# Two-part preparation of the delta rule's chunks, merged loads and a later front, in a two-block kernel

## The chip, the cores and the metric

The kernel runs on one core of one Trainium2 chip, as one launch. The metric is the device time in microseconds from the first to the last instruction, with what lies around it; the core's engines are TensorE (PE, with its weight loads as PEld), VectorE (DVE), ScalarE (ACT), GpSimd (POOL) and SyncE (SP), which issues all DMAs of this kernel.

## What is computed

Two blocks on 1024 tokens of width 1024. The first (a gated delta rule, a dilated attention and a feed-forward part) is the same in both kernels. The second runs twice (two layers), on 256 context and 1024 latent tokens, and is where the change lies:

```python
def _layer(x, ctx, ...):
    h_lat = x * (1.0 + scale) + shift          # the context alike
    ru, rg, aq, ak, av, ag, nq, nk, nv, ng = split(h @ w_in)
    # RWKV-7 on centred conv of ru, forward and backward, 6 heads of 64
    #   S = S*w - (S kk) b + v k;  y = S r
    S_f, S_b, ys_c = _rwkv_bidir(rin_c, S0, S0)
    _, _, ys_l = _rwkv_bidir(rin_l, S_f, S_b)
    yr = _rwkv_output(...)                     # group norm, plus bonus * v
    ya = _block_attention(...)                 # 6 query heads, 2 key heads
    yn = _neighbourhood_attention(...)         # 8 x 16 windows plus context
    y = concat(yr*silu(rg), ya*silu(ag), yn*silu(ng)) @ w_out
    x = _layer_norm(ALPHA * x + gate * y, ln_g, ln_b)
```

The inputs and results are float32. Large products are made from a rounded part and its remainder (three matmuls for one product).

## The kernel before, in words

For each layer, front makes the projections. project computes 10 blocks of 128 recurrent channels: the products land in banks "mm", are evacuated by copies that alternate between ScalarE and VectorE into raw, go through a convolution of three steps on VectorE (cv) and are stored to R in DRAM. For the third of each group of blocks (k) it also makes unit vectors kn at once: squares (sq), a product with hsel (L1356), GpSimd's power (hrs), a broadcast (L1372) and VectorE's product. Beside it factors, a generator of which project takes four steps for each block from the fifth on, works in six slices of 640 tokens: it loads X4 from R, makes tanh factors (L1576, L1578), cumulated decays, and stores the chunks' factors bk and G and the bonus vb (product at L1616). What is left of it is run in project_att. The compiler's scheduler sets the order there.

In stage the order of TensorE, VectorE, ScalarE and GpSimd is the one in which the code writes them: Timeline.run picks, among generators that wait, the one to write next, by its own account of what each engine has done (spend). SP's order is not held to it; the scheduler places the DMAs. The generators are the gate products, attention's scores and values, and the recurrence: scan walks ten steps s, each of a forward and a backward block of 128 tokens, in half-steps of 64, and needs three preparations prep(s, pr), one for each pair of heads. Data of a step lie in one of two slots (G, SK, AB, BT, U).

A prep takes one of four tickets, loads bk, G and vT into the slot (30 DMAs a step), multiplies bk with G (L1889, L1891), masks the results into A, AB and G's other half (L1893 to L1897), adds flips (L149) and inverts A in tri_inverse2: C goes to DRAM (wD) and comes back spread over partitions (wR), GpSimd does 15 steps of forward substitution of two operations each (L436, L438) and the last placing (L440), and TensorE, ScalarE and VectorE join the 16-blocks in five products (L149 to L485). The result is U. launch(s + 2) at the end of step s starts the next three that use this slot.

Attention asks for each query's raw tile with four loads (both, L2064) and for the bias with two.

## Time and profile before

| | us |
|---|---|
| median of 3 runs | 4374.69 |
| lowest, highest | 4362.69, 4382.45 |
| the profiled execution | 4353.97 |
| its span, first to last instruction | 4352.2 |
| TensorE busy in it | 3928.2 |
| mean granted clock of TensorE | 0.948 of full speed |

The granted clock has two levels, 1.2 and 2.4 GHz, shown as 0.5 and 1.0. Block 1 takes up to about 1587 us; then come, for layer 0, the recurrent projection (1668 to 1893), the other projections (to 2085), the gate products with the first preparations (to 2230), the stage of scan and attention (to 2880 and its tail to 2921) and the closing; for layer 1 the same from 3080, with its stage from 3600 to about 4218. A busy TensorE is not TensorE at its peak: a matmul counts as busy at either clock.

### The profile page before, as it was taken

The numbers are of one execution on the slowest core, as the hardware profiler recorded it, in microseconds if no ns is written. First come the engines' busy times: TensorE is split into PE (matmuls) and PEld (weight loads), VectorE is DVE, ScalarE is ACT, GpSimd is POOL, SyncE is SP. The second block draws the span as 40 slices with busy tenths as digits, with TensorE's granted clock in tenths as the row PEclk, the third lists the DMA queues.
The fourth block names the chain that finished last, engine by engine and source line by source line (L and its number), as shares of the span: only waits on it lengthen the run. The fifth ranks groups of instructions, "written<-read, shape, count | busy, mean of one in ns | idle before, by whom it ended". The sixth has DMA issues, their size and how long they took to land.

```text
span 4352.2 us, 91620 instructions
## 1 busy us (share of the span) xinstructions
PE 3928.2 (90%) x36914; PEld 3184.2 (73%) x36914; DVE 2170.0 (50%) x4701; ACT 1451.1 (33%) x2831; POOL 1698.6 (39%) x3201
## 2 busy tenths in 40 slices
PE   8989998999999998979878988899898997998988
PEld 6767777977788877658766766679766875776768
DVE  5634332489212246765235545567576524555546
ACT  4244443421111122331124544452233114554442
POOL 2444333442232234453114443436444323453435
PEclk9999999999999998989989999999998998998989
DMA  3343224445111124453332333454345334234444
GB/s 113 113 139 85 81 74 126 137 149 160 46 45 53 44 71 135 158 192 102 87 92 66 86 73 87 102 160 137 123 159 201 86 94 103 71 75 94 110 106 156
DMA packets 523961, 466.87 MB, mean 107 GB/s; under 512 B 66416, under 2 KB 448656, under 8 KB 523408
## 3 DMA queue, kind: packets, MB, share of 16 engines
q1 hardware_dynamic: 523536, 461.02, 36.3%
q8 instruction: 289, 4.73, 0.5%
q14 instruction: 136, 1.11, 0.1%
HBM read 330.43 MB, written 130.43 MB: 106 GB/s over the span
## 4 chain that ended last, share of the span: by engine, by line
PE 30%; DMA 9%; DVE 7%; POOL 4%; issue 4%; ACT 2%; SPq 1%; POOLq 0%; DVEq 0%; ACTq 0%
PE bank L687 3%; PE bank L744 3%; PE bank L723 3%; DMA wR<-wD 3%; PE bank L243 2%; PE bank L244 2%; PE bank L245 2%; PE bank L1533 1%; PE bank L149 1%; PE bank L1535 1%; PE bank L1534 1%; POOL wX L438 1%; POOL wY L436 1%; DMA wD<-wC 1%; DMA X<-R 1%
## 5 line engine op out<-in xcount | busy, mean ns | idle before, releaser
L154 POOL TENSOR_TENSOR wlo<-wraw,whi 128x1024 fp32r<-128x1024 f32 (+3 forms) x134 | 319.6, 2400 | 560.9 <-ACT whi L153 525.9
L436 POOL TENSOR_TENSOR wY<-wR,wX 128x60 f32<-128x60 f32 (+5 forms) x900 | 233.0, 259 | 428.5 <-DMA wR<-wD 375.9
L691 DVE CUSTOM_DVE_ANT_0 S<-bank,zero 128x256 f32<-128x256 f32 (+1 forms) x372 | 204.7, 558 | 173.6 <-PE bank L687 170.9
L727 ACT COPY PT<-bank 128x512 f32<-128x512 f32 x346 | 202.0, 584 | 236.4 <-PE bank L723 234.4
L153 ACT CAST whi<-wraw 128x1024 fp32r<-128x1024 f32 (+3 forms) x164 | 156.9, 989 | 370.0 <-PE bank L245 163.0
L245 PE MATMUL bank<-h2T,wlo 128*128 128x512 f32 x704 | 278.1, 397 | 0.0
L244 PE MATMUL bank<-h2T,whi 128*128 128x512 f32 x704 | 277.9, 395 | 0.0
L243 PE MATMUL bank<-h2T,whi 128*128 128x512 f32 x704 | 275.9, 394 | 0.3 <-ACT h2T L785 0.3
L438 POOL TENSOR_TENSOR wX<-wX,wY 128x60 f32<-128x60 f32 (+5 forms) x900 | 237.6, 264 | 70.5
L243 PE MATMUL bank<-whi,yh 128*128 128x256 f32 x832 | 241.4, 291 | 17.7 <-ACT yh L153 16.1
L723 PE MATMUL bank<-cst,S 128*128 128x128 f32 x1416 | 233.6, 288 | 19.4 <-ACT S L648 10.2
L244 PE MATMUL bank<-wlo,yh 128*128 128x256 f32 x832 | 240.5, 289 | 3.2 <-DVE wlo L2257 2.8
L744 PE MATMUL bank<-PT,nav 128*64 128x128 f32 (+1 forms) x2832 | 239.4, 290 | 3.4 <-ACT PT L727 3.2
L245 PE MATMUL bank<-whi,yl 128*128 128x256 f32 x832 | 239.5, 289 | 0.8 <-POOL yl L154 0.8
L648 ACT ACTIVATE S<-S,mx 128x1280 f32<-128x1280 f32 (+3 forms) x180 | 202.9, 1127 | 10.3 <-DVE mx L695 8.5
L723 PEld LDWEIGHTS bank<-cst,S 128*128 128x128 f32 x1416 | 161.2, 143 | 57.7 <-ACT PT L727 17.7
L744 PEld LDWEIGHTS bank<-PT,nav 128*64 128x64 f32 (+1 forms) x2832 | 152.2, 139 | 69.3 <-issue 51.8
L415 POOL TENSOR_TENSOR wB<-A,cst 128x256 f32<-128x256 f32 x60 | 43.9, 732 | 406.4 <-DVE A L1893 406.4
L243 PE MATMUL bank<-hT,whi 128*128 128x512 f32 x464 | 190.1, 410 | 10.4 <-ACT sqkv L131 6.7
L244 PE MATMUL bank<-hT,whi 128*128 128x512 f32 x464 | 187.0, 403 | 0.0
L245 PE MATMUL bank<-hT,wlo 128*128 128x512 f32 x464 | 186.0, 401 | 0.0
L1332 DVE CUSTOM_DVE_ANT_0 mj<-wm,cc 128x512 bf16<-128x512 f32 x192 | 179.3, 934 | 8.4 <-POOL cc L1320 3.2
(467 smaller groups left out, 10877.2 us busy)
## 6 DMA issues: line engine op xcount, KB each, us to landing
wraw<-in_w_in SPq DMA_DIRECT2D x86, 512.0 KB
wR<-wD SPq DMA_DIRECT2D x60, 512.0 KB
wm<-in_w_mod SPq DMA_DIRECT2D x96, 256.0 KB
X<-R SPq DMA_DIRECT2D x12, 1280.0 KB
G<-gt SPq DMA_DIRECT2D x24, 640.0 KB
bk<-bk SPq DMA_DIRECT2D x24, 640.0 KB
bk<-bk SPq DMA_DIRECT2D x120, 128.0 KB
G<-G SPq DMA_DIRECT2D x240, 64.0 KB
```

Source lines behind the costliest of these rows:

```text
L154: (eng or self.nc.gpsimd).tensor_tensor(lo, raw, hi.bitcast(F32), ALU.subtract)
L243: nc.tensor.matmul(p, lhsT=lh, rhs=rh, start=kk == 0, stop=False)
L244: nc.tensor.matmul(p, lhsT=lh, rhs=rl, start=False, stop=False)
L245: nc.tensor.matmul(p, lhsT=ll, rhs=rh, start=False, stop=kk == n - 1)
L436: eng.tensor_tensor(t, custom(R, i * 64 + i + 1, [((15 - 2 * i) * 64 + 31 - i, 2), (16, 2), (1, n)]), custom(x, i, [(47 - 2 * i, 2), (16, ...
L438: eng.tensor_tensor(o, o, t, ALU.subtract)
L648: nc.scalar.activation(s[:, :total], s[:, :total], AF.Exp, bias=mx[:, 5:6], accum_out=mx[:, 6:7])
L691: nc.vector.tensor_tensor_reduce(out=s[:, c0:c0 + n], in0=p[:, c0 % 512:c0 % 512 + n], in1=b, scale=1.0, scalar=-3.0e38, op0=ALU.add, op1= ...
L723: nc.tensor.transpose(pt[:rows[i], i], P[h][0][:, c0:c0 + rows[i]], k.ident)
L727: nc.scalar.copy(t[:, :full], pt[:, :full])
L744: nc.tensor.matmul(pv[h * 64:h * 64 + 64, 0], lhsT=V, rhs=t[:V.shape[0], i], start=seen[h] == 1, stop=seen[h] == n)
L1332: nc.vector.tensor_tensor_reduce(out=j, in0=w, in1=cc[:, v, i * 512:i * 512 + 512], scale=1.0, scalar=0.0, op0=ALU.mult, op1=ALU.add, accu ...
```

## The change

- prep is in two parts. Part one takes a ticket, loads bk in one DMA and gk, a second copy of G's columns of 128 partitions, in one, into the tile that wR takes afterwards; multiplies bk with the first half of gk (L1942), masks it into A, and inverts A in its own place. Part two waits for the slot (ready[s]), copies A to U on ScalarE, makes the other products (L1956, L1958), the masks and the flips, and gives the ticket back.
- shared(s) loads a slot's G and vT for all three pairs of heads in 10 DMAs; fill(s + 2) starts it at the end of step s, and the first time in rwkv. The preparations of the next step are launched when the third of a step has its ticket.
- In tri_inverse2 the store of C, the load of wR and GpSimd's steps are steps of the planner of their own.
- The planner counts 0.6 us of SP for each DMA, a queue of 220 KB/us that all share, and 1.8 us after it; before it counted 0.06, 2.0 and 120 KB/us for each alone.
- A query's raw tile takes two loads, a pair of bias tiles one; the query's next load, the stores of attention's results and of the gates each have a step of their own.
- Front: the unit vectors are spread over the next blocks (unit) and written into sq; all evacuations in project go to ScalarE; five tiles t5 instead of four; factors takes the fourth channel block as a tile of its own, leaves each slice's bonus to the next slice, and has banks "f" (6 and 7) while "r" keeps 4 and 5; three of its steps for each block instead of four.

The core of the diff:

```diff
 def project(...):
+    def unit(pr, a, sq):
+        yield
+        norms = heads_rsqrt_bc(k, hp, sq, 0, NT, 1.0, "max", 1e-12, slow=True)
+        next(norms)
+        yield
+        for b0, m, p in norms:
...
+        nc.sync.dma_start(L.R[:, pr * 4 + 2, :], sq[:, 0:1280])
...
-            k.copy(raw[:, o:o + n], p)
+            nc.scalar.copy(raw[:, o:o + n], p)
         dn.chan(w, j % 2 * 128, hT, segs, ev)
+        next(norm, None)
...
-            for _ in range(4):
+            for _ in range(3):
                 next(side, None)
 def tri_inverse2(...):
     nc.vector.tensor_reduce(C, ...)
+    yield "-"
     nc.sync.dma_start(D.rearrange("b j x -> (b j) x"), C.rearrange("p u t -> p (u t)"))
-    R = new("R", (128, 16, 4, 16), 0)
-    nc.sync.dma_start(R, ...)
     eng.tensor_copy(x, ...)
-    yield "-", 1.0
+    yield "-"
+    R = new("R", (128, 16, 4, 16), 0)
+    nc.sync.dma_start(R, ...)
+    yield "-"
 Timeline.spend:
-            t = max(self.at[e], self.now)
-            self.at[e] = t + 0.06
-            self.landed = max(self.landed, t + 2.0 + math.prod(c for _, c in i.outs[0].ap) * 4 / 120e3)
+            t = self.at[e] = max(self.at[e], self.now) + 0.6
+            t = self.at["queue"] = max(self.at["queue"], t) + math.prod(c for _, c in i.outs[0].ap) * 4 / 220e3
+            self.landed = max(self.landed, t + 1.8)
 def rwkv(...):
-    def prep(s, pr):
+    def shared(s):
+        a = s % NS
+        f, b = fwd[s], bwd[s]
+        for h in range(2):
+            for pr in range(3):
+                nc.sync.dma_start(G[a][h][HS[h], pr].rearrange("p (d c) x -> p d (c x)", d=2),
+                                  two(L.G[HS[h], pr, 0, 0, :], f * 256, b * 256, 20 * 128, [(1, 256)]))
+            for d, blk in ((0, f), (1, b)):
+                nc.sync.dma_start(SK[a][h][HS[1 - h], :, 0, d * 2:d * 2 + 2]..., L.vT[:, :, h, blk * 2:blk * 2 + 2]...)
+        yield "-"
+        ready[s] = True
+    def prep(s, pr):
...
         ticket = tickets.pop(0)
+        started[s] += 1
+        if started[s] == 3:
+            launch(s + 1)
...
-                nc.tensor.matmul(p[HS[h], u], lhsT=be[u][HS[h]], rhs=g[h][HS[h], pr, u], start=True, stop=True)
+                nc.tensor.matmul(p[HS[h], u], lhsT=be[u][HS[h]], rhs=gk[HS[h], u, 0:64], start=True, stop=True)
+        A = t1(f"A{ticket}", (128, 4, 64))
+        nc.vector.tensor_tensor(v4(A), v4(p), rm[:, :, :, 0:64], ALU.mult)
+        yield "-"
+        yield from tri_inverse2(k, wk, A, A, ticket, nc.gpsimd)
+        yield "-"
+        while not ready[s]:
+            yield WAIT
+        nc.scalar.copy(U[a][:, pr], A)
+        yield "B", 0.0, None, ("mm", "g")
...
-        rounds.add(flips(a, pr, be, ka), 1 + s * 0.05)
-        yield "-"
-        yield from tri_inverse2(k, wk, A, U[a][:, pr], ticket, nc.gpsimd)
+        yield from flips(a, pr, be, ka)
         tickets.append(ticket)
...
-            launch(s + 2)
+            fill(s + 2)
```

How the order moves, at three places. First SP in layer 0, early in the stage. The numbers behind a name are the buffer: G00 and G01 are slot 0's, refilled for step 2, G10 and G11 slot 1's; wR2 as the output of a load from G0 is gk. Before:

```order
L423 DMA wD_17169<-wC_17167 128x64
L425 DMA wR_17171<-wD_17169 128x1x1024
L2064 DMA qraw_17198<-gqk0_12533 64x128 x4
L2138 DMA ydr0_12536<-rsum_17215 128x128
L423 DMA wD_17238<-wC_17236 128x64
L1879 DMA bk0_18148<-bk0_12537 128x2x128 x2
L425 DMA wR_17240<-wD_17238 128x1x1024
L1879 DMA bk2_18682<-bk0_12537 128x2x128
L1881 DMA G00_15641<-G0_12538 64x256
L1881 DMA G01_15642<-G0_12538 64x256
```

After, from behind a value tile, three vv, a second value tile and the first bias tile:

```order
L2256 DMA nab_23989<-in_rpb 128x2x512
L1932 DMA bk0_16979<-bk0_12537 128x2x256
L1913 DMA G10_16931<-G0_12538 64x2x256 x3
L1916 DMA SK10_16929<-vT0_12531 64x3x128 x2
L1913 DMA G11_16932<-G0_12538 64x2x256 x3
L1916 DMA SK11_16930<-vT0_12531 64x3x128 x2
L1932 DMA bk2_16952<-bk0_12537 128x2x256
L1935 DMA wR2_16954<-G0_12538 128x2x256
L1932 DMA bk3_16956<-bk0_12537 128x2x256
L1935 DMA wR3_16958<-G0_12538 128x2x256
L1935 DMA wR1_17316<-G0_12538 128x2x256
L2183 DMA qraw_17131<-gqk0_12533 64x2x128 x2
L1913 DMA G00_15653<-G0_12538 64x2x256 x3
```

The G of slot 0 stood behind two pairs of wD and wR; now the loads of two slots follow each other, six or ten in one stretch, and the loads that part one needs (bk and gk) stand between them with no wD or wR ahead.

Second TensorE in the same place: the first product of the third preparation that uses slot 0 or, after, of a preparation ahead of its slot. Before:

```order
L744 MATMUL bank4_75<-PT_17404,nav_16845 64x128 x4
L1889 MATMUL bank0_71<-G00_15641,bk3_17376 64x128
L1889 MATMUL bank0_71<-G01_15642,bk3_17376 64x128
L1891 MATMUL bank5_76<-G00_15641,bk3_17376 64x128
L1891 MATMUL bank5_76<-G01_15642,bk3_17376 64x128
```

After:

```order
L748 MATMUL bank4_75<-PT_17252,nav_16927 64x128 x4
L752 MATMUL bank4_75<-cst_63,mx_17217 64x128
L752 MATMUL bank4_75<-cst_63,mx_17223 64x128
L1942 MATMUL bank0_71<-wR2_16954,bk2_16952 64x64 x8
L150 MATMUL bank6_77<-cst_63,bk1_16539 64x64 x2
```

The product that A is made from read G00 and G01 of the slot; it now reads wR2, which is gk, and the flips of another preparation follow it.

Third TensorE at the end of layer 0's recurrent projection (kd0 the bonus, sq and hrs the unit vectors, cv the transposes of v, w2s the tanh factors). Before:

```order
L1576 MATMUL bank6_77<-hid_13075,w2s_13074 128x320 x2
L1616 MATMUL bank4_75<-kd0_13489,cst_63 128x320
L1616 MATMUL bank5_76<-kd0_13489,cst_63 128x320
L1576 MATMUL bank4_75<-hid_13075,w2s_13074 128x320
L1576 MATMUL bank5_76<-hid_13075,w2s_13074 128x320
L1356 MATMUL bank4_75<-cst_63,sq_13730 128x2 x10
L1372 MATMUL bank5_76<-cst_63,hrs_13743 64x128 x8
L1372 MATMUL bank6_77<-cst_63,hrs_13743 64x128 x8
L1372 MATMUL bank4_75<-cst_63,hrs_13743 64x128 x4
L1425 MATMUL bank2_73<-cst_63,cv_13908 128x128 x4
L1425 MATMUL bank3_74<-cst_63,cv_13908 128x128 x2
L1576 MATMUL bank5_76<-hid_13075,w2s_13074 128x320
```

After:

```order
L1587 MATMUL bank6_77<-kd0_13580,cst_63 128x320
L1377 MATMUL bank5_76<-cst_63,hrs_13811 64x128 x3
L1587 MATMUL bank7_78<-kd0_13580,cst_63 128x320
L1377 MATMUL bank5_76<-cst_63,hrs_13811 64x128 x5
L1377 MATMUL bank4_75<-cst_63,hrs_13811 64x128 x3
L1447 MATMUL bank2_73<-cst_63,cv_13815 128x128 x2
L1377 MATMUL bank4_75<-cst_63,hrs_13811 64x128 x2
L1608 MATMUL bank6_77<-hid_13075,w2s_13074 128x320
L1377 MATMUL bank4_75<-cst_63,hrs_13811 64x128 x3
L246 MATMUL bank1_72<-whi_13940,hA01_12151 128x256
L244 MATMUL bank1_72<-whi_13940,hA00_12150 128x256
```

Before, the product with hsel (sq) and its broadcast (hrs) follow each other; after, the product with hsel has gone up among the projection's products, and the broadcast is followed by such products (L246, L244).

## Rows read from the trace of the kernel before

**Rows 1.** The page, part 1: busy us (share of the span) xinstructions.
```profile
PE 3928.2 (90%) x36914; PEld 3184.2 (73%) x36914; DVE 2170.0 (50%) x4701; ACT 1451.1 (33%) x2831; POOL 1698.6 (39%) x3201
```

**Rows 2.** Windows, the projection's two tails: us, engines' busy (xcount), PEclk, DMA share, GB/s.
```profile
1850.50:1895.00 44.50, 24.11 (x104) 15.46 (x102) 27.59 (x32) 13.41 (x23) 25.16 (x16) 0.62 0.55 194
...
3262.00:3305.00 43.00, 25.54 (x116) 17.28 (x115) 27.95 (x31) 10.76 (x20) 24.65 (x16) 0.64 0.54 188
```

**Rows 3.** Windows, gate products and stage of layer 0, then of layer 1.
```profile
2085.00:2230.00 145.00, 133.59 (x1083) 109.30 (x1081) 30.63 (x62) 23.65 (x49) 28.79 (x99) 0.96 0.28 78
2230.00:2880.00 650.00, 548.16 (x9868) 435.87 (x9869) 337.26 (x1131) 305.09 (x669) 262.37 (x915) 0.93 0.36 89
3486.00:3600.00 114.00, 106.76 (x828) 82.97 (x827) 28.87 (x53) 21.35 (x41) 28.00 (x99) 0.97 0.32 92
3600.00:4240.00 640.00, 563.44 (x9841) 444.28 (x9842) 337.36 (x1109) 308.36 (x647) 271.17 (x919) 0.93 0.38 92
```

**Rows 4.** Waits of PE, recurrent projection, project_att, layer 1's projection: us, times, longest.
```profile
PE bank L243 <- DVE raw L133: 6.9, 2, 5.6
...
PE bank L1616 <- DVE kd L1613: 4.4, 3, 1.7
...
PE bank L1356 <- ACT sq L1433: 5.4, 1, 5.4
```

**Rows 5.** Waits of PE in both stages: 2085:2230, then 2230:2880, then 3600:4240.
```profile
PE bank L149 <- POOL wR L440: 6.3, 1, 6.3
...
PE bank L1889 <- DMA G<-G: 26.2, 7, 16.2
...
PE bank L149 <- issue: 9.6, 1, 9.6
PE bank L149 <- POOL wR L440: 9.1, 3, 5.3
PE bank L149 <- DVE G L1897: 7.6, 3, 3.8
...
PE bank L149 <- POOL wR L440: 16.3, 3, 8.4
PE bank L1889 <- DMA G<-G: 6.2, 6, 2.2
```

**Rows 6.** SP in order of time: start us, us, line, operation, tiles.
```profile
2271.19 0.38 SPq L423 DMA_DIRECT2D wD<-wC  x1
2276.72 0.63 SPq L425 DMA_DIRECT2D wR<-wD  x1
...
2286.45 1.74 SPq L1881 DMA_DIRECT2D G<-G  x3
```

**Rows 7.** PE in order of time, in brackets the idle us before and its end.
```profile
2293.86 0.65 PE L1889 MATMUL bank<-G,bk 64*64 64x128 f32 x2 [16.21 <-DMA G<-G]
```

**Rows 8.** The loads of G in layer 0's stage: duration ns min/median/max.
```profile
L1881 SPq DMA_DIRECT2D G<-G x108: 444/588/1408, 2234.2 to 2760.5; - x108
```

**Rows 9.** Groups of PE, 3600:4218: shape, xcount | busy us, mean ns | idle.
```profile
L1889 PE MATMUL bank<-G,bk 64*64 64x128 f32 x432 | 34.5, 287 | 6.3 <-DMA G<-G 6.2
...
L149 PE MATMUL bank<-cst,wR 64*64 64x64 f32 x432 | 19.0, 230 | 17.3 <-POOL wR L440 16.3 <-issue 0.9
```

**Rows 10.** SP's own waits, 2230:2880.
```profile
SPq L2138 <- DVE rsum L756: 44.5, 12, 13.9
...
SPq L425 <- DMA wD<-wC: 39.2, 20, 5.7
```

**Rows 11.** The page, part 5: xcount | busy, mean ns | idle before, releaser.
```profile
L436 POOL TENSOR_TENSOR wY<-wR,wX 128x60 f32<-128x60 f32 (+5 forms) x900 | 233.0, 259 | 428.5 <-DMA wR<-wD 375.9
...
L438 POOL TENSOR_TENSOR wX<-wX,wY 128x60 f32<-128x60 f32 (+5 forms) x900 | 237.6, 264 | 70.5
```

**Rows 12.** Groups of ACT, 1668:1893 and 2230:2880.
```profile
L129 ACT COPY raw<-bank 128x512 f32<-128x512 f32 x10 | 5.8, 584 | 28.5 <-PE bank L245 28.5
...
L467 ACT COPY wF<-bank 128x256 f32<-128x256 f32 x27 | 10.0, 372 | 24.7 <-PE bank L464 24.7
```

More of the change, by code (lines that the diff above doesn't have):

```diff
@@ L1560, in factors, with bonus @@
     nc.sync.dma_start(hid, L.R[:, 12])
+    def bonus(pr, tk, b, v):
+        for x in range(0, N, 320):
+            p = k.bank([128, 320], "f")
+            nc.tensor.matmul(p, lhsT=k.c("same"), rhs=b[:, x:x + 320], start=True, stop=True)
+            nc.vector.tensor_tensor(v[:, x:x + 320], v[:, x:x + 320], p, ALU.mult)
+        nc.sync.dma_start(L.vb[:, pr, tk], v)
+    late = None
     for pr in range(3):
@@ L1613, in factors @@
             nc.vector.scalar_tensor_tensor(b, r, L.rk[:, pc], b, ALU.mult, ALU.mult)
-            for x in range(0, N, 320):
-                p = k.bank([128, 320], "r")
-                nc.tensor.matmul(p, lhsT=k.c("same"), rhs=b[:, x:x + 320], start=True, stop=True)
-                nc.vector.tensor_tensor(v[:, x:x + 320], v[:, x:x + 320], p, ALU.mult)
-            nc.sync.dma_start(L.vb[:, pr, tk], v)
+            late = pr, tk, b, v
             yield
+    bonus(*late)
 def qk_norm(k, wk, p, t, last, L):
@@ L2113, in ask @@
         landed, rounds.landed = rounds.landed, 0.0
-        for h in range(2):
-            both(raw[:, h], src[h])
+        for i in range(2):
+            nc.sync.dma_start(raw[i * 64:i * 64 + 64], src)
         rounds.read()
```

114 lines of the change are left out of this document (66 added, 48 removed).

## The prediction

> **What bounds the kernel now.** I read the page's first part, then the windows stage by stage, then who waited for whom on TensorE, and last the SP queue row by row around the longest wait. TensorE is busy for 3928.2 us of 4352.2 [rows 1], so what a change can give back is its idle time and the time at the lower clock level. Block 1 keeps its order, so I look only at the two layers of block 2, in two kinds of place.
>
> First, the end of the recurrent projection (project and factors). In 44.5 us of layer 0 and 43.0 of layer 1, TensorE is busy for 24.11 and 25.54 us, at a granted clock of 0.62 and 0.64 of full speed [rows 2]. No projection product stands between the small matmuls there. 24.11 x 0.62 is 15 us of work at full clock, 25.54 x 0.64 is 16; the rest, 29 and 27 us, is waiting and low clock.
>
> Second, the two stages in which scan and attention share TensorE. Span less TensorE's busy time is 11.4, 101.8, 7.2 and 76.6 us in the four windows, 197 in all; their clock of 0.96, 0.93, 0.97 and 0.93 makes another 145 x 0.04 + 650 x 0.07 + 114 x 0.03 + 640 x 0.07 = 100 us that full speed would not have used if TensorE worked all the time [rows 3]. Two causes stand out [rows 5]: the first product of a preparation waits for G (26.2 and 6.2 us, group A), and the first flip of an inverse waits for GpSimd's forward substitution (6.3, 9.1 and 16.3, and once 9.6 that the view calls issue, at the same instruction: 41.3, group B). The longest wait of A is 16.21 us [rows 7], and SP's queue shows why [rows 6]: wD is issued at 2271.19, then SP stands until 2276.72 before wR can go, and only at 2286.45, after the next pair of the same kind, does it come to the loads of G. The loads wait behind other transfers' semaphores.
>
> **The change, part by part.** *Front.* The unit vectors' product with hsel and its broadcast now come one product group and two later, the bonus matmuls come behind the next slice's first tanh, factors has banks of its own (6 and 7), and all evacuations of project go to ScalarE. In the new order on TensorE the tail keeps 8 tanh matmuls, 20 broadcasts, 10 transposes and 2 bonus matmuls with only 14 products between; its hsel products and most tanh matmuls have moved up among runs of some 20 products. I leave the 15 and 16 us of work and 8 us of waiting for each tail: 29 - 8 = 21 and 27 - 8 = 19, together 40 off. Around it stand waits of the same kind, 6.9 us for raw, 4.4 for the bonus in the next section and 5.4 for sq in layer 1 [rows 4], 17 in all; half of it is 8 off. Three steps of side work per column block instead of four push about a fifth of factors into project_att: 3 us on. ScalarE's extra copies, some 40 in all, I cost at nothing: it is busy for 13.41 us of the tail's 44.5 [rows 2]; uncovered, they would cost 584 ns each [rows 12], 23 us. Front: -45 us, bounds -70 and -10.
>
> *SP.* A slot took 6 loads of bk, 12 of G and 12 of vT; it now takes 3, 3 (gk, the copy of G that the inverse reads), 6 and 4: 14 fewer, for 20 slots 280. Each of the 90 queries takes 2 loads of raw instead of 4 (180), the bias 16 fewer. That is 476 issues at 0.588 us [rows 8], 280 us of SP time. Also wD and wR are now two steps of the planner with a pause between, and stores of attention and gates have one ahead of them, so SP stands less in front of an unfinished write: it stood 39.2 us for wD and 44.5 for rsum in the first stage alone [rows 10]. What is queued behind a waiting SP is every load; that is how A comes about. Of A's 32.4 us I take 22 off, not all: in the new order the value tile, three vv, a second value tile and two bias tiles stand ahead of slot 1's loads, so its first part two may still wait.
>
> The Trainium skill says the opposite of the last paragraph's premise: on the page DMA: Bandwidth & Descriptors, section Issuing engines are not separate DMA queues, the sequencer's time to start a DMA is called usually small relative to the DMA itself. Here an issue of 64 KB takes SP 0.588 us, and 108 of them stand in one stage [rows 8], so the trace disagrees; by the rule the merging would save nothing, and A and half of B would stay.
>
> *The inverse ahead.* Before, a preparation could not start until the slot's G was free, and each slot's three then shared GpSimd in a burst: 470.6 us of L436 and L438 over 60 preparations are 7.8 us each, and 375.9 us were waited for wR [rows 11]. Now the product for A reads gk, loaded into the tile that wR takes later, so three inverses can begin as tickets come free, and only part two (AB, G's lower half, the flips) waits for the slot. TensorE then waits less often on GpSimd; but there are still four tickets, now held until the flips are done, and GpSimd does the same work. I take half of B, 21 us.
>
> *Clock.* A and B together lose 43 of 197 us of idle time, 22%; the same share of the 100 us is 22 off.
>
> *What it adds.* The product be x G is done in two halves: 960 rows of 64x128 at 34.5/432 = 80 ns become 1920 of 64x64 at 19.0/432 = 44 ns [rows 9]: 84 - 77 = 8 us on, on the engine that bounds. A copy of the inverse into U costs ScalarE 372 ns [rows 12], 60 times 22 us, beside other work; it stands ahead of part two's products, so uncovered it costs at most that. Below nothing it can't fall. New waits: at the start of the first scan the order has two half-steps with only pieces of inverses between, where before scores and values stood; the nearest wait on an evacuation is 7.6 us in three times [rows 5], 2.5 us each, and I put three of them, 7 us, for both layers, bounds 0 and 30.
>
> *Stage sum:* -22 - 21 - 22 + 8 + 7 = -50; bounds -130 (A and B gone, half the other idle time covered, clock with it) and +10. Total -95 on the profiled run's 4353.97, which is 4259. The median of the runs shown, 4374.69, lies 20.7 above the profiled run, so the forecast is 4280.
>
> **The rivals.** *More than counted.* Part two is short, so each slot is ready early and the planner has attention to place at all times: both lower bounds, -70 and -130, give 4175; half way to it from the forecast is 4228. For it: 197 idle microseconds, most of them beside preparations. Against: the new order puts about as many attention matmuls into each slot's period as the old.
>
> *SP is not what holds the loads.* Then A and half of B stay: -95 + 22 + 10 = -63, 4312, less the clock's part in it, some 10: 4322. This is what the skill's rule gives. For it: G's waits are only 32 us of 197. Against: rows 6.
>
> *Nothing gained.* The stalls move: an engine that is in order waits at the next thing that the planner timed wrong. Only the front's tail in part (-25) stays and the rest is given back: 4350 to 4375. For it: group B is a wait on GpSimd, and GpSimd's work is the same.
>
> *Slower.* The flips write bank 5, in which part two's second product has just been made, so a flip waits until VectorE has taken that product out: 7.6 us in three times in the first stage [rows 5], 2.5 us each. In the new order flips follow part two within one group of matmuls at several places. If every one of the 60 stood 2.5 us, that is 150 us for the 8 of now: -95 + 150 - 8 = +47, 4422, and with the clock after it 4440. It decides from 95/60 = 1.6 us for each preparation. Against it: VectorE has one product fewer to take out before the flips than now, and the planner knows when a bank is free.
>
> **How the numbers follow.** Forecast (4240 to 4330) 0.50; more than counted 0.15; SP not the cause 0.13; nothing gained 0.12; slower 0.10. Differences under 0.5%, 22 us, a measurement can hardly tell from none. Faster by more: 0.50 + 0.15 + 0.13 = 0.78; the same 0.12; slower 0.10. The range 4200 to 4370 leaves out the end of the first rival (0.05), the slower one and a part of the fourth.
>
> **What would show it.** Right: the two tails shorten from 44.5 and 43.0 to about 25; G's waits fall under 12 us over both stages and L150's on wR to about 20; the gap of 16.21 has no successor; the clock of the stages rises to 0.95. Wrong: TensorE waits for wR<-G or bk at L1942, or for G at L1958, by tens of microseconds (the hoisted value and bias loads), or flips (L150) wait for G on VectorE in most preparations. If the stages' idle time stays at 197 while SP's issues fall, SP was never the cause.

## The result, and the profile after

The changed kernel takes 4251.3 us (median of 4 runs, 4238.57 to 4256.43), the kernel before 4368.69 beside it (4351.8 to 4382.45): ratio 0.9725, with a 95% interval of 0.9696 to 0.9753. The forecast was 4280, from 4200 to 4370. The profiled execution of the change took 4248.21 us, 105.8 less than the 4353.97 of before.

The time is told best by sections that begin and end at the same work in every kernel: from the first product of the recurrent projection to the last product of the other projections (the two fronts), from there to the first product of the closing (the stages, gate products included), and the closing of layer 0 up to the next projection. These are starts and ends of matmuls in the profiled executions:

| us | before | after | difference |
|---|---|---|---|
| front of layer 0 | 418.7 | 399.8 | -18.9 |
| stage 0 | 833.2 | 766.2 | -67.0 |
| closing 0 | 161.3 | 172.1 | +10.9 |
| front of layer 1 | 406.2 | 388.1 | -18.1 |
| stage 1 | 750.7 | 740.8 | -9.8 |
| the rest (block 1, closing 1) | 1782.2 | 1779.4 | -2.8 |

Stage 0 and its closing belong together, since attention's last tiles now run beside the first products of the closing. Block 1, which is the same in every kernel of this study, took 1660.8 to 1673.3 us up to the first projection; so I give no weight to a section's difference of less than some 8 us.

The busy times of the page's first part, of the kernel after, to be read beside [rows 1]:

```profile
PE 3917.6 (92%) x37874; PEld 3187.5 (75%) x37874; DVE 2140.2 (50%) x4664; ACT 1487.6 (35%) x2928; POOL 1705.8 (40%) x3201
```

Windows of the kernel after: the two projections' ends, from the last long run of products to the next (beside [rows 2]), then gate products and stage of each layer (beside [rows 3]). The columns are the window, its length, then busy time and count of PE, PEld, DVE, ACT, POOL, the granted clock, the share of the DMA engines and GB/s:

```profile
1858.30:1878.40 20.10, 15.12 (x86) 8.81 (x84) 17.57 (x18) 9.27 (x18) 13.53 (x10) 0.82 0.60 200
3192.80:3216.50 23.70, 15.66 (x80) 9.87 (x79) 19.18 (x22) 8.44 (x17) 12.68 (x8) 0.70 0.64 214
2064.80:2205.00 140.20, 135.08 (x1183) 110.09 (x1183) 38.21 (x79) 26.31 (x55) 36.98 (x132) 0.99 0.33 98
2205.00:2831.00 626.00, 567.40 (x10491) 453.67 (x10487) 352.73 (x1200) 329.78 (x730) 262.72 (x889) 0.97 0.44 107
3391.20:3500.00 108.80, 99.77 (x753) 77.51 (x751) 33.39 (x65) 20.50 (x38) 29.57 (x88) 0.98 0.37 110
3500.00:4132.10 632.10, 565.23 (x10377) 449.55 (x10377) 339.00 (x1107) 314.84 (x676) 271.88 (x929) 0.94 0.42 101
```

The ends are down from 44.5 and 43.0 us to 20.1 and 23.7. TensorE's idle time in the four windows of the stages is 5.1 + 58.6 + 9.0 + 66.9 = 139.6 us. The clock of layer 0's stage has risen to 0.97; layer 1's is at 0.94, hardly above the 0.93 of before.

Waits of TensorE in the kernel after, first from 2064.8 to 2831, then from 3391.2 to 4132.1 (us in all, times, longest; beside [rows 5]; L150 is the flip, L1942 the product for A, L1956 and L1958 part two):

```profile
PE bank L727 <- ACT PT L731: 11.5, 5, 8.7
PE bank L691 <- DVE mx L695: 6.8, 5, 5.1
PE bank L150 <- POOL wR L444: 4.1, 5, 1.5
...
PE bank L150 <- DVE G L1962: 3.0, 5, 1.7
...
PE bank L150 <- issue: 2.3, 1, 2.3
...
PE bank L1956 <- DVE y L2088: 0.6, 1, 0.6
```

```profile
PE bank L150 <- POOL wR L444: 15.5, 3, 10.7
PE bank L150 <- DVE G L1962: 3.3, 3, 1.5
...
PE bank L150 <- issue: 1.7, 2, 0.9
...
PE bank L1942 <- DMA bk<-bk: 0.4, 1, 0.4
```

In layer 0 attention's own waits are at the top now, and part two waits for 1.1 us in two places (0.6 us for VectorE at L1956, 0.5 for ScalarE at L1958). In layer 1 the longest is still a wait for GpSimd, 10.7 us. Group A, the waits for a load at the first product, has gone from 32.4 us to 0.4. Group B (GpSimd, with what the view calls issue) has gone from 41.3 to 4.1 + 2.3 + 15.5 + 1.7 = 23.6. SP's DMA issues take 266 us in stage 0 (407 before) and 232 in stage 1 (367 before).

What is left in layer 1 is its end. Window of the kernel after, from attention's last product to the closing:

```profile
4087.00:4132.10 45.10, 27.42 (x423) 21.86 (x417) 14.99 (x35) 8.61 (x19) 9.53 (x14) 0.72 0.28 75
```

Attention is done at 4087.2, the recurrence at 4129.0: for 42 us TensorE has only the scan's last step and its norms to do, and the clock is at 0.72. Before, that tail was 24 us long (4209.3 to 4233.1). In layer 1 the recurrence ends the stage, which I take to be why it gained so little; seats5 and mixed_costs below bear on it.

### The profile page after: what moved, and what is told of

It is laid out like the page before. It is cut to its first block, busy times and chain, and to the rows that moved or that the text cites. A ratio compares the mean times of both kernels' runs of the same rounds, so it can differ in the third digit from the quotient of the medians.

```text
span 4246.4 us, 93025 instructions
## 1 busy us (share of the span) xinstructions
PE 3917.6 (92%) x37874; PEld 3187.5 (75%) x37874; DVE 2140.2 (50%) x4664; ACT 1487.6 (35%) x2928; POOL 1705.8 (40%) x3201
## 2 busy tenths in 40 slices
DMA packets 513406, 482.66 MB, mean 114 GB/s; under 512 B 58929, under 2 KB 441169, under 8 KB 512849
## 5 line engine op out<-in xcount | busy, mean ns | idle before, releaser
L440 POOL TENSOR_TENSOR wY<-wR,wX 128x60 f32<-128x60 f32 (+8 forms) x900 | 233.1, 259 | 255.4 <-DMA wR<-wD 202.4
L246 PE MATMUL bank<-h2T,wlo 128*128 128x512 f32 x704 | 278.0, 397 | 0.0
L244 PE MATMUL bank<-h2T,whi 128*128 128x512 f32 x704 | 275.9, 394 | 0.3 <-ACT h2T L790 0.3
L442 POOL TENSOR_TENSOR wX<-wX,wY 128x60 f32<-128x60 f32 (+8 forms) x900 | 239.9, 267 | 70.5
L244 PE MATMUL bank<-whi,yh 128*128 128x256 f32 x832 | 240.8, 290 | 16.0 <-ACT yh L154 14.9
L727 PE MATMUL bank<-cst,S 128*128 128x128 f32 x1416 | 229.0, 284 | 16.2 <-ACT PT L731 13.6
L246 PE MATMUL bank<-whi,yl 128*128 128x256 f32 x832 | 238.9, 288 | 0.8 <-POOL yl L155 0.8
L244 PE MATMUL bank<-hT,whi 128*128 128x512 f32 x464 | 190.2, 410 | 9.2 <-ACT sqkv L132 6.7
L727 PEld LDWEIGHTS bank<-cst,S 128*128 128x128 f32 x1416 | 158.5, 141 | 53.3 <-ACT PT L731 25.1
L246 PE MATMUL bank<-hT,wlo 128*128 128x512 f32 x464 | 185.7, 400 | 0.0
```

Source lines behind the costliest of these rows:

```text
L244: nc.tensor.matmul(p, lhsT=lh, rhs=rh, start=kk == 0, stop=False)
L246: nc.tensor.matmul(p, lhsT=ll, rhs=rh, start=False, stop=kk == n - 1)
L440: eng.tensor_tensor(t, custom(R, i * 64 + i + 1, [((15 - 2 * i) * 64 + 31 - i, 2), (16, 2), (1, n)]), custom(x, i, [(47 - 2 * i, 2), (16, ...
L442: eng.tensor_tensor(o, o, t, ALU.subtract)
L727: nc.tensor.transpose(pt[:rows[i], i], P[h][0][:, c0:c0 + rows[i]], k.ident)
```

## The experiments

Sections of every kernel that was run, from one profiled execution each (us); the ratio is that of the runs to the kernel before, with its interval. The two can differ: the profiled execution of before is 3 to 15 us under the medians beside which the ratios are taken, those of unmerged and slot_first are 12 and 11 us over their own.

| kernel | both fronts | stage 0 with closing | stage 1 | ratio |
|---|---|---|---|---|
| before | 824.9 | 994.4 | 750.7 | 1 |
| the change | 787.9 | 938.3 | 740.8 | 0.9725 (0.9696 to 0.9753) |
| front_only | 782.0 | 990.1 | 746.8 | 0.9848 (0.9829 to 0.9867) |
| stage_only | 833.2 | 947.6 | 745.4 | 0.9864 (0.9833 to 0.9895) |
| merged_before | 831.3 | 951.3 | 724.0 | 0.9842 (0.9822 to 0.9863) |
| unmerged | 787.3 | 1001.3 | 798.5 | 0.9988 (0.9971 to 1.0006) |
| front_merged | 778.9 | 946.6 | 725.6 | 0.9720 (0.9681 to 0.9759) |
| slot_first | 778.0 | 998.5 | 786.2 | 0.9955 (0.9938 to 0.9972) |
| old_costs | 779.6 | 984.2 | 706.2 | 0.9753 (0.9732 to 0.9774) |
| act_query | 788.0 | 951.6 | 737.3 | 0.9767 (0.9738 to 0.9796) |
| one_step | 780.7 | 951.4 | 732.8 | 0.9788 (0.9762 to 0.9814) |
| seats5 | 781.4 | 970.8 | 712.5 | 0.9732 (0.9686 to 0.9778) |
| mixed_costs | 783.6 | 935.8 | 714.2 | 0.9676 (0.9638 to 0.9714) |
| late_seats | 789.1 | 935.3 | 711.2 | 0.9676 (0.9656 to 0.9697) |

In the stages front_only, merged_before and front_merged have the order of the kernel before on TensorE, VectorE, ScalarE and GpSimd, stage_only and unmerged that of the change, mixed_costs and late_seats that of the change in layer 0. slot_first, old_costs, act_query, one_step and seats5 give the planner another problem, and their traces show another order throughout both stages; what they measure is the thing tried together with the plan that comes of it.

### The two halves of the change, each alone

**front_only** is the kernel before with the change's front, **stage_only** the change with the front of before. The edit of the first, cut to its core:

```diff
+FRONT = {"mm": FULL[0] + FULL[1], "a": FULL[2] + FULL[3], "r": FULL[4] + FULL[5], "f": FULL[6] + FULL[7]}
...
+                norm = unit(pr, a, sq)
+                next(norm)
...
-            for _ in range(4):
+            for _ in range(3):
                 next(side, None)
...
+            late = pr, tk, b, v
```

> The kernel before with the front of the change alone (unit vectors spread over later blocks, bonus a slice later, evacuations on ScalarE, banks f, three steps instead of four); preparations, loads and planner are those of before. In the two traces the two fronts give 418.7 to 399.8 and 406.2 to 388.1 us, 37 together. Theory (the parts add up, the front's gain stays): 34 to 40 us under the kernel before, ratio 0.991, and the two projections' ends lose most of their low clock. Rival (what the front gives is taken back where the stage's first preparations wait for loads that now come sooner): ratio 0.996 or more, with the stages longer by 15 us or more.

> The change with the front of before: two-part preparations, merged loads, the new steps and costs of the planner. Theory (the parts add up): the traces' stages give 833.1 to 766.2 and 750.7 to 740.9 us, 76.7, of which the first closing takes 10.8 back: 62 to 82 us under the kernel before, ratio 0.981 to 0.986. The prediction's own term for it was 50 (ratio 0.989). Rival (the stage needs the front's earlier stores of bk, G and vb): ratio 0.990 or more, with waits for wR<-G or bk at the first preparations.

Measured: 4298.6 and 4308.08 us beside 4361.89, ratios 0.9848 and 0.9864. In the sections the front alone gives 42.9 us in the fronts and 8 in the stages, to which I give no weight; by the ratio it is worth 66 us, more than the theory's 34 to 40, and the sections do not say where the rest lies. The other half gives 46.8 in stage 0 with its closing and 5.3 in stage 1, and 59 us by its ratio, a little under the theory's 62. Both rivals fall, and the parts add up: 0.9848 x 0.9864 is 0.9714, and the change is at 0.9725. Nothing that can be measured is taken back where the two meet, so each half can be judged by itself.

### Merging alone, and the change without merging

**merged_before** is the kernel before with fewer, larger loads. The planner counts a merged load as the ones that it replaces, so that the order on the four engines stays the same in both stages. One thing comes with it: bk lies in another order in DRAM, so that a preparation's piece is contiguous, and the packets of the page fall from 523961 to 495987 at nearly the same bytes (466.87 and 466.78 MB).

```diff
-        for d, blk in ((0, f), (1, b)):
-            nc.sync.dma_start(bk[:, d], L.bk[:, pr, d, :, blk * 128:blk * 128 + 128])
-            for h in range(2):
-                nc.sync.dma_start(g[h][HS[h], pr, d * 2:d * 2 + 2], L.G[HS[h], pr, d, blk * 2:blk * 2 + 2])
-                nc.sync.dma_start(sk[h][HS[1 - h], pr, 0, d * 2:d * 2 + 2], L.vT[:, pr, h, blk * 2:blk * 2 + 2])
+        for h in range(2):
+            rounds.merged(2, g[h][HS[h], pr].rearrange("p (d c) x -> p d (c x)", d=2), two(L.G[HS[h], pr, 0, 0, :], ...))
+            rounds.merged(2, sk[h][HS[1 - h], pr, 0].rearrange("p (d c) x -> p d (c x)", d=2), two(L.vT[:, pr, h, 0, :], ...))
+            if h == 0:
+                rounds.merged(2, bk.rearrange("p d i t -> p d (i t)"), two(L.bk[:, pr, 0, 0, 0, :], ...))
...
-        for h in range(2):
-            both(raw[:, h], src[h])
+        for i in range(2):
+            rounds.merged(2, raw[i * 64:i * 64 + 64], src)
```

> The kernel before, its order on the four engines kept, with its loads merged alone: a preparation takes 5 loads instead of 10, a query 2 instead of 4, a pair of bias tiles 1 instead of 2, about 496 issues fewer; one-part preparations as before. Theory (SP's issues are what holds the loads back): TensorE's wait for G falls from 32 us to under 16 over both stages and the time by 16 to 40 us, ratio 0.991 to 0.996. Rival (the issues cost nothing: SP stands for wD and for stores, and an engine in order stands with it): G's wait stays at 25 us or more, ratio 0.998 to 1.002.

**unmerged** is the reverse: the change, with every merged load but gk taken apart again and counted by the planner as one. It keeps the change's order of bk in DRAM, and its packets differ from the change's almost only in those under 512 B (67568 and 58929), so that here the number of DMAs alone is altered.

```diff
-        for i in range(2):
-            nc.sync.dma_start(raw[i * 64:i * 64 + 64], src)
+        for i in range(2):
+            rounds.several([(raw[i * 64:i * 64 + 64, h], src[:, h]) for h in range(2)])
...
-                nc.sync.dma_start(G[a][h][HS[h], pr].rearrange("p (d c) x -> p d (c x)", d=2), two(L.G[HS[h], pr, 0, 0, :], ...))
+                parts(*((G[a][h][HS[h], pr, d * 2:d * 2 + 2], L.G[HS[h], pr, d, blk * 2:blk * 2 + 2]) for d, blk in ((0, f), (1, b))))
```

> The change with its loads taken apart again and its order on the four engines kept: a slot's 10 loads become 24, a preparation's bk 2, a query's raw tile 4, a pair of bias tiles 2, about 536 issues more; the planner counts them as before. Theory (SP's issues are what holds the loads back): TensorE waits again for G, gk or bk by 20 us or more over both stages, and the time goes up by 20 to 50 us, ratio to the kernel before 0.977 to 0.984. Rival (the two parts made the loads early enough, and what an issue costs is hidden): no such wait over 6 us, ratio 0.970 to 0.975 as the change.

Measured: merged_before 4296.87 beside 4361.89, ratio 0.9842; unmerged 4354.66, ratio 0.9988. Both went past what the theory gave them. Some 500 issues fewer, at the same bytes and the same order of work, are worth 43.1 us in stage 0 with its closing and 26.7 in stage 1: 70 in all, and 69 by the ratio. Put back into the change, the issues cost it 63.0 and 57.7 us, and with them everything that it had won, the front's gain too. Its plan does not know of them; whether one that did would lose less, no run shows.

Waits of TensorE in merged_before, 2230 to 2888:

```profile
PE bank L1906 <- DMA G<-G: 16.8, 3, 14.0
PE bank L149 <- DVE G L1914: 8.3, 4, 3.8
```

and in unmerged, 2205 to 2892:

```profile
PE bank L691 <- DVE mx L695: 18.1, 3, 17.6
PE bank L727 <- ACT PT L731: 12.8, 6, 7.6
PE bank L1956 <- DMA bk<-bk: 11.8, 4, 5.5
PE bank L150 <- POOL wR L444: 7.2, 4, 2.7
PE bank L1956 <- DMA wR<-G: 6.5, 3, 4.2
```

In unmerged the loads of bk and gk are waited for again, 18.3 us here, and 3.9 in the gate products before and 17.1 in layer 1 besides; the transposes and scores (L727, L691) wait too. In merged_before one long wait for G is left (14.0 us), against the theory, by which G would be waited for less than 16 us in both stages: it is 17.6. The waits for G don't hold most of its gain. A good part of it is in what GpSimd waits for. Waits of GpSimd in stage 0: before, merged_before, after, one fence each:

```profile
POOL wY L436 <- DMA wR<-wD: 199.0, 27, 17.2
```

```profile
POOL wY L436 <- DMA wR<-wD: 159.3, 26, 13.9
```

```profile
POOL wY L440 <- DMA wR<-wD: 94.7, 23, 13.1
```

The load of wR stands in SP's queue like all others. With fewer issues ahead of it GpSimd starts sooner, and with GpSimd the flip that TensorE waits for: L149 on wR, with what the view calls issue, has gone from 25.0 us in layer 0's windows to 4.5 in merged_before. Group B, which the prediction had put down to the three preparations that share GpSimd in a burst, was in good part SP's.

What one issue takes, by the instructions of a line: first the G loads of 64 KB before (240 of them), then those of 128 KB after (120) (duration ns, min/median/max):

```profile
L1881 SPq DMA_DIRECT2D G<-G x240: 444/588/1467, 2085.8 to 4126.6; - x120
```

```profile
L1913 SPq DMA_DIRECT2D G<-G x120: 573/598/1870, 2060.3 to 4002.2; - x120
```

Twice the bytes take SP 598 ns instead of 588, and bk's 256 KB take it 377. What is paid is the issue, and not by its bytes; why bk's is shorter stays open.

### Is the two-part preparation worth anything?

**front_merged** has the front of the change and the merged loads, but one-part preparations and the old planner: front_only and merged_before in one kernel.

```diff
+    k.places = FRONT
...
+        for h in range(2):
+            rounds.merged(2, g[h][HS[h], pr].rearrange("p (d c) x -> p d (c x)", d=2), two(L.G[HS[h], pr, 0, 0, :], ...))
```

> The kernel before with the change's front and with its loads merged, one-part preparations and the old planner: the two parts that were tried alone, together. Theory (front and merging are the whole gain, the two-part preparation and the planner's new steps add nothing): the sections of the two runs add up to 43 + 69 = 112 us under the kernel before, ratio 0.971 to 0.978, within 10 us of the change. Rival (the inverse ahead is worth at least the 21 us that the prediction gave it): ratio 0.979 or more, since it is missing here.

Measured: 4226.6 us beside 4356.96, ratio 0.9720 (0.9681 to 0.9759), the same as the change. Three of its four runs lie at 4223.1 to 4229.63 and one at 4257.72, which makes the interval wide; by the medians it is 0.9701, where the change is 0.9731. Its stages and closing take 946.6 + 725.6 = 1672.2 us, the change's 938.3 + 740.8 = 1679.1. It has the stages' order of the kernel before. So the two-part preparation, gk, the loads shared by three pairs and the planner's new steps and costs together gave nothing that can be measured; the theory holds, and if anything they cost a little.

**slot_first** is the change with the inverse started only when its slot has landed:

```diff
-        while not tickets:
+        while not (tickets and ready[s]):
             yield WAIT
         ticket = tickets.pop(0)
```

> The change, but a preparation takes its ticket only when its slot's loads have landed, so that no inverse starts ahead; everything else as in the change. Theory (starting ahead is worth something): 20 to 50 us over the change, ratio to the kernel before 0.977 to 0.984, with steps of the scan 3 to 5 us longer each. Rival (four tickets, each held for some 80 us from the load to the last flip, set the pace, 3 x 80 / 4 = 60 us a step, and an inverse that may begin earlier only waits for a ticket): within 10 us of the change, ratio 0.970 to 0.975.

Measured: 4337.4 us, ratio 0.9955. That is 100 us over the change by the ratios ((0.9955 - 0.9725) x 4357), more than the theory's 20 to 50, and the rival falls. The starts of the scan's steps show how: from step 1 to step 9 they are 67.0 and 67.7 us apart in layer 0 and layer 1, against 55.6 and 61.3 in the change and 60.8 and 59.8 in merged_before. Attention is then done long before the recurrence. Windows of slot_first, from the end of attention to that of the recurrence:

```profile
2825.30:2897.20 71.90, 50.42 (x804) 40.88 (x804) 19.49 (x51) 13.79 (x34) 18.96 (x55) 0.63 0.25 68
4094.00:4231.30 137.30, 95.53 (x1904) 79.81 (x1898) 44.19 (x110) 25.10 (x64) 64.72 (x213) 0.70 0.34 81
```

By the mean times of its pieces a preparation in the change takes 57.0 us from A to the inverse in layer 0, and 13.7 more for the copy, part two's products and the flips, which the one-part form makes beside the inverse (before: 64.7 us, and nothing behind it). So I read the two runs together: starting ahead pays for what stands behind the inverse, and without it that lengthens every step; the two parts give back what they cost, and no more. That the 13.7 us are what makes slot_first's steps longer is argued, not shown.

### The planner's account, its steps, and ScalarE's queue

**old_costs**: the account of a load as before.

```diff
-            t = self.at[e] = max(self.at[e], self.now) + 0.6
-            t = self.at["queue"] = max(self.at["queue"], t) + math.prod(c for _, c in i.outs[0].ap) * 4 / 220e3
-            self.landed = max(self.landed, t + 1.8)
+            t = max(self.at[e], self.now)
+            self.at[e] = t + 0.06
+            self.landed = max(self.landed, t + 2.0 + math.prod(c for _, c in i.outs[0].ap) * 4 / 120e3)
```

> The change with the planner's account of loads as before: 0.06 us of SP each, 2.0 us after, 120 KB/us for each alone. Theory (the new account puts the products of a preparation behind the landing of its loads): waits of TensorE for wR<-G, bk or G of 20 us or more and 20 to 40 us over the change, ratio 0.977 to 0.982. Rival (with the merged loads the account matters little): within 10 us of the change, ratio 0.970 to 0.975.

Measured: 4249.97 us, ratio 0.9753 (0.9732 to 0.9774), which lies between the two. The sum hides two large differences: stage 0 with its closing is 45.9 us longer than in the change, and stage 1 is 34.6 shorter. Waits of TensorE in old_costs, 2060 to 2840:

```profile
PE bank L1942 <- DMA bk<-bk: 23.8, 4, 15.5
PE bank L1942 <- DMA wR<-G: 9.3, 2, 8.4
```

In layer 0 the theory's waits are there (33.1 us), and attention ends 68 us after the recurrence has, against 29 in the change. In layer 1 there is only one of 2.8 us, and recurrence and attention end 2 us apart (702.4 and 700.3 us after the gate products began) where the change has 737.8 and 696.0.

**one_step**: the store of C and the load of wR in one step again.

```diff
     tmp = new("Y16", (128, 4, 16))
-    yield "-"
     R = new("R", (128, 16, 4, 16), 0)
```

> The change with the store of C (wD) and the load of wR again in one step of the planner, as before the change. Theory (two steps of their own let SP do other loads between, as the prediction has it): SP stands longer for wD than the 48.5 us of layer 0's stage, and 10 to 30 us over the change, ratio 0.975 to 0.980. Rival (SP is placed by the scheduler and stands for wD in either form: 43.7 us before the change, 48.5 with it): within 10 us, ratio 0.970 to 0.975.

Measured: 4263.93 us, ratio 0.9788 (0.9762 to 0.9814), 0.6% over the change. SP's own waits, of one_step from 2060 to 2830 and of the change from 2064.8 to 2831:

```profile
SPq L431 <- DMA wD<-wC: 75.8, 29, 6.1
```

```profile
SPq L432 <- DMA wD<-wC: 48.5, 25, 7.7
```

SP stands longer for wD in the joined form, as the theory says. The times agree less well: the profiled execution (4243.48) shows none of it, and stages and closing add up to 1684.3 us against 1679.1, so the size, 13 us by the medians and 27 by the ratios, stays uncertain. The order on the engines is another too, so the difference is not shown to be that of the two steps.

**act_query**: the 180 loads of queries issued by ScalarE.

```diff
-            nc.sync.dma_start(raw[i * 64:i * 64 + 64], src)
+            nc.scalar.dma_start(raw[i * 64:i * 64 + 64], src)
```

> The change with the 180 loads of queries issued by ScalarE's queue instead of SP's. Theory (SP's issues still hold the loads back, at the price that the merging showed, 69 us for 496 issues or 0.14 us each): 15 to 30 us under the change, ratio 0.966 to 0.969. Rival (with SP issuing for 297 us of the first stage's 766 there is room, and ScalarE pays some 0.6 us for each issue, 108 us in all, between the evacuations that TensorE waits for): no gain or up to 20 us over the change, ratio 0.972 to 0.977.

Measured: 4254.17 us, ratio 0.9767 (0.9738 to 0.9796): no gain. The instructions of the line:

```profile
L2183 ACTq DMA_DIRECT2D qraw<-gqk x108: 581/610/1597, 2202.7 to 3821.1; - x108
```

An issue takes ScalarE's queue 610 ns, 110 us for 180, and ScalarE is the engine that copies attention's transposed scores (PT), for which TensorE waits: 20.7 us in layer 1's stage, 2.1 in the change. What SP's queue was relieved of is paid there, at least in part; how much the other order of the engines takes or gives, the run doesn't separate. Fewer issues helped; the same number, part of them from another engine, did not.

### What layer 1's stage is bound by

**seats5** gives a ticket back when its inverse is made. Five seats hold bk and A until the flips, and one tile of the norms (gsq) has two buffers instead of three to make room.

```diff
-        ticket = tickets.pop(0)
+        ticket, seat = tickets.pop(0), seats.pop(0)
...
         yield from tri_inverse2(k, wk, A, A, ticket, nc.gpsimd)
+        tickets.append(ticket)
...
         yield from flips(a, pr, be, ka)
-        tickets.append(ticket)
+        seats.append(seat)
```

> The change with a ticket given back when its inverse is made, not when the flips are done: the tiles of bk and A come from five seats that are held until the flips, the inverse's own tiles from the four tickets (gsq has two buffers instead of three, for the room). Theory (in layer 1 the preparations' pace is the bound: the scan's steps start 3 to 7 us after their last part two, and a ticket is held for some 13 us after its inverse): steps fall from 61.3 to under 56 us in layer 1, the recurrence's tail behind attention (41.8 us) shrinks, 15 to 35 us under the change, ratio 0.964 to 0.969. Rival (GpSimd's and the dependent products' waits inside the chain set the pace, four inverses at a time whatever the tickets): steps within 2 us, ratio 0.970 to 0.976.

Measured: 4243.76 us, ratio 0.9732 (0.9686 to 0.9778), no different from the change as a whole. But layer 1 does nearly what the theory says: the scan's steps are 56.0 us apart instead of 61.3 (the theory had under 56), the recurrence ends 3 us after attention instead of 42, and the stage takes 712.5 us, 28.3 less. Layer 0 loses 32.5 us in stage and closing, where attention now ends 40 us after the recurrence, 29 in the change: there the recurrence wasn't the bound.

**mixed_costs** keeps the change's layer 0 and gives layer 1 the old account; **late_seats** gives layer 1 the five seats as well.

```diff
-            tl, homes = Timeline(k), Homes(ep)
+            tl, homes = Timeline(k, last), Homes(ep)
...
+            if self.old:
+                t = max(self.at[e], self.now)
+                self.at[e] = t + 0.06
+                self.landed = max(self.landed, t + 2.0 + math.prod(c for _, c in i.outs[0].ap) * 4 / 120e3)
+                return
```

> The change with the planner's old account of loads in layer 1's stage alone and the new in layer 0's. In the two traces stage and closing of layer 0 give 938.3 with the new account and 984.2 with the old, stage 1 740.8 and 706.2. Theory (what a stage takes is set by its own plan, and the account only decides how recurrence and attention share the time): the better of each adds up, 25 to 40 us under the change, ratio 0.963 to 0.968. Rival (layer 1's gain of the old account hangs on what layer 0 left behind): ratio 0.970 or more.

> The change with layer 1's stage alone altered: the old account of loads, and five seats with the ticket given back after the inverse. With the old account alone layer 1's recurrence ended 710.5 us after the start of its gate products and attention 708.4. Theory (they end together, so TensorE's own work is the bound there and a faster recurrence brings nothing): within 8 us of the kernel with the old account in layer 1, ratio 0.965 to 0.970. Rival (the scan's steps of 58.6 us still hold the stage): steps under 55 us and 10 to 25 us less, ratio 0.961 to 0.965.

Measured: 4218.57 us beside 4357.1, ratio 0.9676 (0.9638 to 0.9714), and 4218.7 beside 4362.19, ratio 0.9676 (0.9656 to 0.9697). The better plan of each layer adds up, and these are the fastest kernels of the study, 0.5% under the change by the ratios. The window of layer 1's stage in mixed_costs, its last 25.4 us and then the whole from gate products to closing:

```profile
4080.00:4105.40 25.40, 20.06 (x243) 15.12 (x241) 12.16 (x40) 13.53 (x28) 5.96 (x7) 0.97 0.40 112
3391.20:4105.40 714.20, 656.88 (x11128) 521.65 (x11126) 368.24 (x1170) 335.26 (x715) 301.07 (x1015) 0.97 0.42 107
```

Recurrence and attention end 2 us apart in it (710.5 and 708.4 us), and its clock is 0.97 where the change has 0.98 and 0.94 in the two windows. The five seats shorten the steps further, to 54.8 us, and in late_seats the recurrence ends 694.1 us after the gate products began, well ahead of attention's 720.3; the stage's time stays. So once both end together, a faster recurrence brought nothing here.

## Why the prediction was right, point by point

**Front, forecast -45 us: right in sum.** The fronts gave 37.0 us in the change and 42.9 alone. The two ends, forecast at 21 + 19 us, gave 24.4 and 19.3 by their windows. They hold 15.12 and 15.66 us of busy TensorE at a clock of 0.82 and 0.70, which is 12 and 11 us of work at full clock, less than the 15 and 16 that the step left there. The step's other terms are less sure. The waits for raw, for which it took half off, fell from 6.9 to 1.5 us in layer 0, but those for sq, which ScalarE makes, rose: 7.3 us in layer 0, none before, and 8.8 in layer 1, 5.4 before [rows 4]. So it is not shown that the evacuations on ScalarE cost nothing; no run tried them by themselves.

**SP, forecast -22 us for the loads: right about the queue, wrong about where its effect ends.** The step priced the issues right: 476 at 0.588 us are 280, and SP's DMA issues in both stages take 276 us less. It then allowed them only the one wait in which a load of G was the last to come. merged_before shows what they were worth: 70 us. Of these only 14.8 are waits for G (32.4 to 17.6); 25.1 are waits of group B, and the rest lies in other waits and in the clock, 0.96 and 0.95 over the two stages where it was 0.94 and 0.93. The step that failed is that who waits last on TensorE was taken for the whole effect. A shorter queue also brings wR to GpSimd sooner, and queries to ScalarE (which waited for them 19.7 us in layer 0 before and 11.7 in merged_before), and through these chains TensorE.

The step's second half did not come true: SP does not stand less in front of unfinished writes. Its waits for rsum and for wD in layer 0, gate products and stage, before and after:

```profile
SPq L2138 <- DVE rsum L756: 48.4, 15, 13.9
...
SPq L425 <- DMA wD<-wC: 43.7, 23, 5.7
```

```profile
SPq L2206 <- DVE rsum L760: 70.1, 22, 8.1
...
SPq L432 <- DMA wD<-wC: 48.5, 25, 7.7
```

**The Trainium skill's rule** (DMA: Bandwidth & Descriptors, section Issuing engines are not separate DMA queues) is that the time to start a DMA is usually small relative to the DMA itself. For one DMA the trace agrees with it, and the prediction read it wrongly: in [rows 6] and [rows 7] the product starts 7.4 us after the first of the loads of G was issued, and an issue takes 0.588 us. What the prediction made of the rule, that merging would then save nothing, does not follow from it: the starts of one queue add up, and some 500 of them were worth 70 us at the same bytes.

**The inverse ahead, forecast -21 us for group B: the sum right, the reason wrong.** Group B fell by 17.7 us (41.3 to 23.6), but merging alone took it to 16.2 by the same count (4.1 + 0.4 in layer 0's windows, 10.8 + 0.9 in layer 1's), with the preparations still one-part and three in a burst. Waits of TensorE in merged_before, layer 0 and then layer 1:

```profile
PE bank L149 <- POOL wR L440: 4.1, 2, 3.0
...
PE bank L149 <- issue: 0.4, 1, 0.4
```

```profile
PE bank L149 <- POOL wR L440: 10.8, 3, 8.4
...
PE bank L149 <- issue: 0.9, 1, 0.9
```

So the burst on GpSimd wasn't the main cause of it, and front_merged is as fast as the change without any inverse ahead.

**Clock, forecast -22: too small.** By the prediction's own formula the low clock costs 140.2 x 0.01 + 626.0 x 0.03 + 108.8 x 0.02 + 632.1 x 0.06 = 60 us in the stages after, against 100. The idle time fell by more than the step had, 57 of 197 us (29%) instead of 43, and that the same share of the low clock would go was the wrong step: it fell by 40%. In layer 0's stage before, the longest stretch at the lower level (17.1 us from 2281.0) begins within TensorE's longest wait (16.21 us, to 2293.86) and outlasts it; in that stage after, no such stretch is longer than 10.2 us.

**The split product, forecast +8: right.** In layer 1 the rows of L1889 and L1891 were busy for 37.8 + 35.4 = 73.2 us; those of L1958, L1956 and L1942 are busy for 78.0, 4.8 more. In layer 0 it is 74.3 and 75.0 us, 0.7 more: 5.5 for both.

Groups of TensorE in layer 1 before, 3486.2 to 4237, and after, 3391.2 to 4132 (beside [rows 9]):

```profile
L1889 PE MATMUL bank<-G,bk 64*64 64x128 f32 x480 | 37.8, 286 | 6.3 <-DMA G<-G 6.2
L1891 PE MATMUL bank<-G,bk 64*64 64x128 f32 x480 | 35.4, 286 | 0.2 <-DVE G L1897 0.2
```

```profile
L1958 PE MATMUL bank<-G,bk 64*64 64x128 f32 x480 | 35.4, 290 | 1.1 <-DVE G L1962 1.1
...
L1956 PE MATMUL bank<-G,bk 64*64 64x64 f32 x480 | 21.7, 232 | 1.5 <-DVE y L2088 0.6 <-DVE A L1944 0.5 <-DVE AB L1959 0.3
L1942 PE MATMUL bank<-wR,bk 64*64 64x64 f32 x480 | 20.9, 225 | 2.5 <-issue 2.0 <-DMA bk<-bk 0.4
```

**New waits, forecast +7: not there in this form.** Part two's products wait for 2.6 us in all of layer 1, and the flips' wait for VectorE fell (3.0 and 3.3 us, from 20.2 in both stages before). The hoisted value, vv and bias loads, which the prediction feared ahead of slot 1's, made no product wait.

**What was missing** is the stage's own bound. The prediction added waits of TensorE, and never asked which of the two chains, attention or recurrence, ends a stage. In layer 0 attention does, and every wait that went could be worth its time and the clock behind it. In layer 1 the recurrence does, and there the change gained 9.8 us where merging alone had gained 26.7. The total came out right in part by luck: merging brought far more than its term, the inverse ahead nothing that can be measured, and layer 1's end took a part back. The signs that the prediction named came true (ends of 20.1 and 23.7 us, 0.4 us of waits for the loads, 19.6 for wR), but they do not say which part brought it: in merged_before, without any inverse ahead, the wait for wR is already down to 14.9 us. Only merged_before and front_merged tell the causes apart.

**The rivals.** SP not what holds the loads: refuted twice, by merged_before and by unmerged. More than counted: not reached by the change. Nothing gained: what the two parts do by themselves, since front_merged is as fast without them. Slower, by flips that stand for VectorE from 1.6 us a preparation on: it was 6.3 / 60 = 0.1 us.

## What to carry to other kernels

Where one queue issues all loads, count its issues before its bytes: merging loads without touching the order of work gave 1.6% here, and taking the merging out of a finished change, with a plan that did not know of it, took all its gain. A wait on an engine that itself waits for a load is a wait on the queue; follow it one step further before giving the gain to another part of the change. And where two chains share an engine, look which ends the stage before adding up waits: once both ended together, a faster recurrence brought nothing, and a planner's costs that suit one stage can be wrong for the next.

## What the runs showed of the hardware

An issue on SP takes 588 ns for 64 KB and 598 for 128 KB (G before and after) and 377 ns for 256 KB (bk after), and on ScalarE's queue 610 ns for 64 KB (act_query): it does not go by the bytes. A product of 128 columns made as two of 64 keeps TensorE busy for 20.9 + 21.7 = 42.6 us instead of 37.8 in layer 1, 13% more for twice the instructions (41.4 instead of 38.0 in layer 0). At the end of layer 1's stage, with a TensorE that is busy for 27.42 of 45.10 us, the granted clock is 0.72; in mixed_costs, with attention beside the recurrence to the end, TensorE is busy for 20.06 of the last 25.40 us at 0.97.
